# First stage of a one-layer encoder block: row scaling, transposes, the last block of w_ada and the later modulation sums

## The chip, the cores and the metric

The kernel runs on one core of a Trainium2 chip. The metric is the device time in microseconds (us). A core has TensorE (PE in the profile, with PEld for its weight loads), VectorE (DVE), ScalarE (ACT), GpSimd (POOL) and SyncE (SP). Each engine works through its own queue in order, and DMAs are issued from the queues of SP, ScalarE and GpSimd. TensorE runs at one of two levels, 1.2 or 2.4 GHz; the profile gives the granted clock as a share of the upper one.

## The reference, cut to what matters

One sequence of 1024 rows of 1024 values, all float32, one layer:

```
mod = silu(c) @ w_ada + b_ada                    # 6 pieces of 1024: shift_m, scale_m, gate_m, shift_f, scale_f, gate_f
h   = rms_norm(x, g_norm_mix) * (1 + scale_m) + shift_m
p   = h @ w_in                                   # 1024 -> 5632
z   = sigmoid(gA) * fourier(p) + sigmoid(gB) * conv(p)
x   = x + gate_m * (z @ w_o)
h2  = rms_norm(x, g_norm_moe) * (1 + scale_f) + shift_f
x   = x + gate_f * expert_choice_moe(h2)         # 16 SwiGLU experts, 128 rows each
out = rms_norm(x, g_final)
```

`rms_norm` divides each row by the root of its mean square. The change is in how `h` comes about and in the sums for the four later pieces of `mod`.

## The kernel before

The products of the block are done in parts: a float32 operand is split into two fp32r parts, the rounded value (`split`, line 94, a copy on ScalarE) and the rest (line 95, a subtraction on VectorE), and three fp32r products stand for one. A plain fp32 matmul stands in the trace as two records. The projection with `w_in` works on four quarters of `h` (two halves of the rows by two halves of the columns) and their sums.

**The ramp** (`ramp`, lines 116 to 257) makes `h`, transposed, and the first products. The rows come in eight tiles of 128 (`load_x`, line 130, into four buffers `x`), first tiles 0 to 3, later 4 to 7. For each tile `norm` squares it on ScalarE with the sum of the row as a second output (line 136), `rstd` (lines 662 to 669) takes one step on VectorE and a power on GpSimd, and VectorE makes a diagonal matrix of the 128 factors (line 139). `turn` (line 145) multiplies a 128x128 block of the tile with that diagonal on TensorE, which transposes and scales it at once; four row tiles fill one PSUM bank of two (`sm`). ScalarE takes it from there (lines 204, 221 and 241).

Beside that stands **the modulation**. `load_ada` (line 152) loads the columns of `w_ada` for shift and scale, half of them at a time, in eight blocks of 128 rows (512 KB each) through the six buffers `ld` that the blocks of `w_in` (`load_pair`, line 280) use too. `ada` multiplies each block by its column of `cact` = silu(c) and adds it to `acc` on VectorE (lines 160 and 162). `modulation` then sums `acc` over the partitions with eight fp32 products with a column of ones (line 170), and three small operations on VectorE make `shift` and `scale` (lines 173 to 175). `shape` (lines 180 to 186) applies them and splits the result, `halfprod` (line 191) runs the products. `consts` (lines 624 to 653) loads `c` and the other vectors, transposes them and computes `cact` (line 646).

The order of the program text in the ramp: `x` 0 to 3, `norm` of them, `ada(0)`, the turn of all eight column blocks, two blocks of `w_in`, `x` 4 to 7, `modulation(0)`, `shape` and products of the first quarter, `norm` of tiles 4 to 7, `ada(1)`, the turn of four column blocks and their products, two blocks of `w_in`, `modulation(1)`, and the second halves.

**The later sums.** In the gate stage `ada_rest` (lines 362 to 381) does the same for each of the other four pieces of `mod` (`q` 0 to 3): eight blocks of `w_ada` added up in `acc` on VectorE (line 372), two fp32 products of a column of ones with 512 columns of `acc` each (line 378), a copy on ScalarE (line 380) and a store to `mod_d`. Each `q` is spread over two calls of `gate`, and its products stand behind those of the second one.

What sets the order: a planner places the instructions of each engine's queue, by the program text where several are ready in its own estimate, and otherwise by readiness; a tile has to wait until a buffer of its name is free. `issue_after` pins an instruction behind another in the queue of one engine. On the chip each queue runs in the order that was planned.

Of the kernel before, what the change touches and what calls it, by code (L numbers as in the profile page):

```python
# [6 lines left out]
F32 = mybir.dt.float32  # L7
F32R = mybir.dt.float32r
# [7 lines left out]
P = 128  # L16
D = 1024
# [11 lines left out]
NSH = 0  # L29
TURN = 10  # L30
# [52 lines left out]
class Block:  # L83
# [32 lines left out]
    def ramp(self, pool, tmp):  # L116
# [11 lines left out]
        def load_x(t):  # L128
            x = tmp.tile([P, D], F32, name="x", bufs=4)
            nc.sync.dma_start(out=x, in_=io["x"][0, t * P:(t + 1) * P, :])  # L130
            return x

        def norm(x):
            sq = tmp.tile([P, D], BF16, name="sq")
            ss = pool.tile([P, 1], F32, name="ss", bufs=4)
            nc.scalar.activation(sq, x, AF.Square, accum_out=ss)
            rs = self.rstd(pool, ss, "x")
            d = pool.tile([P, P], F32, name="diag", bufs=4)
            nc.vector.tensor_scalar(d, self.ident, rs, None, op0=OP.mult)
            return x, d  # L140

        def turn(xs, k):
            ps = self.pss.tile([P, 512], F32, name="sm")
            for i, (x, d) in enumerate(xs):
                nc.tensor.matmul(ps[:, i * P:(i + 1) * P], lhsT=x[:, k * P:(k + 1) * P], rhs=d, start=True, stop=True)
# [10 lines left out]
        def ada(h):  # L156
            acc = tmp.tile([P, 2, 512], F32, name="acc", bufs=2)
            for k, w in enumerate(load_ada(h)):
                if k == 0:
                    nc.vector.tensor_scalar(acc, w, self.cact[:, 0:1], None, op0=OP.mult)  # L160
                else:
                    nc.vector.scalar_tensor_tensor(acc, in0=w, scalar=self.cact[:, k:k + 1], in1=acc,
                                                   op0=OP.mult, op1=OP.add)
            return acc

        def modulation(h, acc):
            ps = self.pss.tile([P, 512], F32, name="sm")
            for a in range(2):
                for j in range(4):
                    nc.tensor.matmul(ps[:, 4 * a + j:4 * a + j + 1], lhsT=acc[:, a, j * P:(j + 1) * P],  # L170
                                     rhs=self.ones[:, 0:1], start=True, stop=True)
            hs = slice(4 * h, 4 * h + 4)
            nc.vector.tensor_tensor(B[:, hs], ps[:, 0:4], self.bada[:, hs], op=OP.add)
            nc.vector.tensor_tensor(A[:, hs], ps[:, 4:8], self.bada[:, 8 + 4 * h:12 + 4 * h], op=OP.add)
# [187 lines left out]
    def ada_rest(self, pool, q):  # L362
# [12 lines left out]
        row = pool.tile([1, D], F32, name="acc")  # L375
        for i in range(2):
            ps = self.pss.tile([P, 512], F32, name="sm")
            nc.tensor.matmul(ps[0:1, :], lhsT=self.ones[:, 0:1], rhs=acc[:, i * 512:i * 512 + 512],
                             start=True, stop=True)
            nc.scalar.activation(row[:, i * 512:(i + 1) * 512], ps[0:1, :], AF.Copy)  # L380
# [1164 lines left out]
```

## Time and profile before

| | us |
|---|---|
| median of 3 runs | 1931.37 |
| lowest and highest of them | 1930.61, 1934.88 |
| the profiled execution | 1933.76 |
| its span in the trace | 1932.00 |
| TensorE busy in the span | 1883.5 (97%) |
| VectorE busy | 1575.3 (82%) |
| ScalarE busy | 1136.2 (59%) |
| GpSimd busy | 312.2 (16%) |

The span is the time between the first and the last instruction of the trace; 1.76 us of the profiled execution lie around it. Engines work at the same time, so the shares don't add up. A stage is bound by what ends last in it, and that is read from the chain of waits and from the busy times of the stage, not from the shares of the whole span. The ramp takes about the first 90 us, the projections go on to 490, Fourier part and mixing to about 800, the experts to the end. Matmuls are pipelined: the length of a record is longer than the distance between two of them.

### The profile page before, as it was taken

To read this page: it belongs to the slowest core of one execution; us is meant where nothing else is said; L and a number is where in the kernel's file an instruction comes from. 1 tells how busy PE (TensorE), PEld (TensorE's weight loads), DVE (VectorE), ACT (ScalarE), POOL (GpSimd) and SP (SyncE) were. 2 spreads that over 40 slices of the span, in tenths; PEclk is the share of its full clock that TensorE was granted. 3 is DMA by queue.
4 is the path that set the end of the run, shared out by engine and by line. 5 is a ranking of instruction groups with operands and counts; after the bars stand their busy time and mean duration, and the time that the engine had idled before them with its cause. 6 is when DMAs were issued, how large, how long until landed. Compare 5 with 4: busy or idle time off the path is not lost.

```text
span 1932.0 us, 24182 instructions
## 1 busy us (share of the span) xinstructions
PE 1883.5 (97%) x8777; PEld 1517.6 (79%) x8777; DVE 1575.3 (82%) x1973; ACT 1136.2 (59%) x1371; POOL 312.2 (16%) x124
## 2 busy tenths in 40 slices
PE   6999999999999999999899999999999999999996
PEld 5788888777788777877788888888888888888884
DVE  5976678676764766999898998998998998899896
ACT  5533333443510423777677776877877777777684
POOL 1000000000130110100000312321330330331231
PEclk9999999999999999999999999999999999999998
DMA  8322224466673862999899999999999999999967
GB/s 289 119 88 66 88 65 143 143 213 230 211 265 126 267 230 77 377 369 360 332 379 358 373 371 383 379 368 378 380 374 367 383 376 372 378 377 375 388 244 305
DMA packets 180236, 549.03 MB, mean 284 GB/s; under 512 B 12644, under 2 KB 51652, under 8 KB 180116
## 3 DMA queue, kind: packets, MB, share of 16 engines
q1 hardware_dynamic: 164736, 494.50, 68.3%
q0 software_dynamic: 14528, 52.75, 8.5%
q8 instruction: 69, 1.13, 0.2%
q14 instruction: 51, 0.42, 0.1%
q10 hardware_dynamic: 852, 0.24, 0.1%
HBM read 507.61 MB, written 39.86 MB: 283 GB/s over the span
## 4 chain that ended last, share of the span: by engine, by line
PE 88%; issue 4%; DVE 3%; DMA 2%; ACT 1%; POOL 1%; ACTq 0%; POOLq 0%; SPq 0%; DVEq 0%
PE a L1225 18%; PE u L1225 17%; PE y L1225 17%; PE pb L317 9%; PE pa L317 6%; PE pc L317 6%; PE mm L114 3%; PE mm L108 3%; PE mm L111 3%; PE tp L1240 1%; PE pa L191 1%; PE pb L191 1%; DMA raw<-in_w_down_e_dram 1%; DMA xg<-h_d,idx 1%; PE tp L1106 1%
## 5 line engine op out<-in xcount | busy, mean ns | idle before, releaser
L95 DVE TENSOR_TENSOR wlo<-raw,whi 128x1024 fp32r<-128x1024 f32 x759 | 883.8, 1218 | 20.3 <-ACT whi L94 18.5
L94 ACT ACTIVATE whi<-raw 128x1024 fp32r<-128x1024 f32 x759 | 777.6, 1059 | 143.5 <-PE a L1225 56.7
L1306 POOL DMA_INDIRECT x_d<-ys,idx x15 | 212.1, 14141 | 505.0 <-DVE ys L1305 479.1
L1225 PE MATMUL a<-whi,xl 128*128 128x512 f32 x512 | 162.4, 399 | 0.0
L1225 PE MATMUL a<-whi,xh 128*128 128x512 f32 x512 | 161.7, 397 | 0.2 <-ACT xh L94 0.2
L1225 PE MATMUL u<-wlo,xh 128*128 128x512 f32 x512 | 161.6, 397 | 0.0
L1225 PE MATMUL y<-whi,hth 128*128 128x512 f32 x496 | 161.4, 402 | 0.0
L1225 PE MATMUL a<-wlo,xh 128*128 128x512 f32 x512 | 161.3, 397 | 0.0
L1225 PE MATMUL u<-whi,xh 128*128 128x512 f32 x512 | 160.5, 395 | 0.0
L1225 PE MATMUL u<-whi,xl 128*128 128x512 f32 x512 | 160.3, 394 | 0.0
L1225 PE MATMUL y<-wlo,hth 128*128 128x512 f32 x496 | 157.3, 397 | 1.4 <-DVE wlo L95 1.4
L1225 PE MATMUL y<-whi,htl 128*128 128x512 f32 x496 | 157.9, 398 | 0.3 <-DVE htl L95 0.3
L94 ACT ACTIVATE wh<-s 128x512 fp32r<-128x512 f32 x80 | 50.3, 631 | 134.7 <-PE pc L317 71.4
L1225 PEld LDWEIGHTS a<-whi,xh 128*128 128x128 f32 x512 | 96.4, 189 | 22.7 <-ACT xh L94 0.5
L1225 PEld LDWEIGHTS a<-wlo,xh 128*128 128x128 f32 x512 | 96.5, 189 | 22.2
L1225 PEld LDWEIGHTS u<-whi,xl 128*128 128x128 f32 x512 | 96.4, 188 | 21.6
L1225 PEld LDWEIGHTS u<-whi,xh 128*128 128x128 f32 x512 | 96.1, 188 | 21.5
L1225 PEld LDWEIGHTS y<-wlo,hth 128*128 128x128 f32 x496 | 92.8, 188 | 25.0 <-DVE wlo L95 2.9
L1225 PEld LDWEIGHTS a<-whi,xl 128*128 128x128 f32 x512 | 95.6, 189 | 21.4 <-DVE xl L95 0.4
L1225 PEld LDWEIGHTS u<-wlo,xh 128*128 128x128 f32 x512 | 95.5, 188 | 20.8
L1225 PEld LDWEIGHTS y<-whi,htl 128*128 128x128 f32 x496 | 92.3, 188 | 21.6 <-DVE htl L95 0.7
L1225 PEld LDWEIGHTS y<-whi,hth 128*128 128x128 f32 x496 | 91.8, 188 | 20.5 <-issue 0.5
(530 smaller groups left out, 3176.1 us busy)
## 6 DMA issues: line engine op xcount, KB each, us to landing
raw<-in_w_down_e_dram SPq DMA_DIRECT2D x128, 1024.0 KB, 10.9
raw<-in_w_up_e_dram SPq DMA_DIRECT2D x126, 1024.0 KB, 7.7
raw<-in_w_gate_e_dram SPq DMA_DIRECT2D x124, 1024.0 KB, 7.0
ld<-in_w_ada_dram SPq DMA_DIRECT2D x48, 512.0 KB, 4.7
ld<-in_w_in_dram SPq DMA_DIRECT2D x44, 512.0 KB, 4.5
sg_d<-q POOLq DMA_DIRECT2D x8, 1024.0 KB, 6.0
ld<-sg_d SPq DMA_DIRECT2D x16, 512.0 KB, 4.0
x<-in_x_dram SPq DMA_DIRECT2D x8, 512.0 KB, 5.2
```

Source lines behind the costliest of these rows:

```text
L94: a = self.nc.scalar.activation(hi, src, AF.Copy).ins
L95: self.last = a, self.nc.vector.tensor_tensor(lo, src, hi, op=OP.subtract).ins
L108: nc.tensor.matmul(o, lhsT=lh, rhs=rh, start=first, stop=False)
L111: nc.tensor.matmul(o, lhsT=lh, rhs=rl, start=False, stop=False)
L114: nc.tensor.matmul(o, lhsT=ll, rhs=rh, start=False, stop=last)
L191: nc.tensor.matmul(ps, lhsT=x[:, k, :], rhs=y[:, k, :], start=first and k == 0 and i == 0, stop=not first and k == 3 and i == 2)
L317: nc.tensor.matmul(o, lhsT=x[:, k, :], rhs=y[:, k, :], start=first and k == 0 and i == 0, stop=last and k == 3 and i == 2, skip_group_chec ...
L1106: nc.tensor.transpose(pt[:, k, :], xg[:, (4 * hf + k) * P:(4 * hf + k + 1) * P], self.ident)
L1225: nc.tensor.matmul(o[:, a:b], lhsT=x, rhs=y[:, a:b], start=first and i == 0, stop=end and i == 2)
L1240: nc.tensor.transpose(pt[:, i, :], hs[q // 2][:, 512 * (q % 2) + i * P:512 * (q % 2) + (i + 1) * P], self.ident)
L1306: nc.gpsimd.indirect_dma_start(out=self.x2_d, out_offset=bass.IndirectOffsetOnAxis(ap=idx[:, 0:1], axis=0), in_=ys, in_offset=None, comput ...
```

## The change

- `consts`, `norm`: SiLU of `c` is pinned ahead of the squares on ScalarE.
- `load_x`: the buffer `x` is there seven times instead of four.
- `norm`, `turn`: instead of a diagonal on VectorE and a product with it, ScalarE scales the row tile in place, and TensorE transposes it with the identity.
- `ada`, `modulation`: VectorE adds up seven of the eight blocks of `w_ada` (`NPE` = 7). The last block goes through TensorE as it is, with its column of `cact` as the moving operand (eight fp32 products), into a PSUM tile of its own, and the products of `acc` with the column of ones into another. VectorE adds the first to `b_ada`, and the second to that.
- `ada_rest`: `acc` is split in two fp32r parts, half of the columns at a time, and each half has two fp32r products with a column of ones in fp32r instead of one in fp32.

```diff
--- before.py
+++ after.py
@@ -27,6 +27,7 @@
 NRA, NRB, NRC, NWO = 7, 4, 1, 6
 NWS, NWB = 3, 6
 NSH = 0
+NPE = 7
 TURN = 10
 NCMP = 2
 FIN = ((8, 0), (7, 2), (5, 4), (4, 6))
@@ -126,23 +127,24 @@
         B = self.cpool.tile([P, KD], F32, name="shift")
 
         def load_x(t):
-            x = tmp.tile([P, D], F32, name="x", bufs=4)
+            x = tmp.tile([P, D], F32, name="x", bufs=7)
             nc.sync.dma_start(out=x, in_=io["x"][0, t * P:(t + 1) * P, :])
             return x
 
         def norm(x):
+
             sq = tmp.tile([P, D], BF16, name="sq")
             ss = pool.tile([P, 1], F32, name="ss", bufs=4)
-            nc.scalar.activation(sq, x, AF.Square, accum_out=ss)
+            with self.tc.issue_after(self.cact_ins):
+                nc.scalar.activation(sq, x, AF.Square, accum_out=ss)
             rs = self.rstd(pool, ss, "x")
-            d = pool.tile([P, P], F32, name="diag", bufs=4)
-            nc.vector.tensor_scalar(d, self.ident, rs, None, op0=OP.mult)
-            return x, d
+            nc.scalar.activation(x, x, AF.Copy, scale=rs)
+            return x
 
         def turn(xs, k):
             ps = self.pss.tile([P, 512], F32, name="sm")
-            for i, (x, d) in enumerate(xs):
-                nc.tensor.matmul(ps[:, i * P:(i + 1) * P], lhsT=x[:, k * P:(k + 1) * P], rhs=d, start=True, stop=True)
+            for i, x in enumerate(xs):
+                nc.tensor.transpose(ps[:, i * P:(i + 1) * P], x[:, k * P:(k + 1) * P], self.ident)
             return ps
 
         def load_ada(h):
@@ -154,24 +156,31 @@
                 yield w
 
         def ada(h):
+
             acc = tmp.tile([P, 2, 512], F32, name="acc", bufs=2)
+            rest = []
             for k, w in enumerate(load_ada(h)):
                 if k == 0:
                     nc.vector.tensor_scalar(acc, w, self.cact[:, 0:1], None, op0=OP.mult)
-                else:
+                elif k < NPE:
                     nc.vector.scalar_tensor_tensor(acc, in0=w, scalar=self.cact[:, k:k + 1], in1=acc,
                                                    op0=OP.mult, op1=OP.add)
-            return acc
-
-        def modulation(h, acc):
-            ps = self.pss.tile([P, 512], F32, name="sm")
-            for a in range(2):
-                for j in range(4):
-                    nc.tensor.matmul(ps[:, 4 * a + j:4 * a + j + 1], lhsT=acc[:, a, j * P:(j + 1) * P],
-                                     rhs=self.ones[:, 0:1], start=True, stop=True)
+                else:
+                    rest.append((w, self.cact[:, k:k + 1]))
+            return rest + [(acc, self.ones[:, 0:1])]
+
+        def modulation(h, parts):
             hs = slice(4 * h, 4 * h + 4)
-            nc.vector.tensor_tensor(B[:, hs], ps[:, 0:4], self.bada[:, hs], op=OP.add)
-            nc.vector.tensor_tensor(A[:, hs], ps[:, 4:8], self.bada[:, 8 + 4 * h:12 + 4 * h], op=OP.add)
+            b = [self.bada[:, hs], self.bada[:, 8 + 4 * h:12 + 4 * h]]
+            for n, ps in enumerate((parts[:-1], parts[-1:])):
+                t = self.pss.tile([P, 512], F32, name="sm")
+                for a in range(2):
+                    for j in range(4):
+                        for i, (w, v) in enumerate(ps):
+                            nc.tensor.matmul(t[:, 4 * a + j:4 * a + j + 1], lhsT=w[:, a, j * P:(j + 1) * P], rhs=v,
+                                             start=(i == 0), stop=(i == len(ps) - 1))
+                for a, o in enumerate((B, A)):
+                    nc.vector.tensor_tensor(o[:, hs], t[:, 4 * a:4 * a + 4], o[:, hs] if n else b[a], op=OP.add)
             nc.vector.scalar_tensor_tensor(A[:, hs], in0=A[:, hs], scalar=1.0, in1=self.gmix[:, hs],
                                            op0=OP.add, op1=OP.mult)
 
@@ -373,11 +382,16 @@
             if k % 4 == 3:
                 yield
         row = pool.tile([1, D], F32, name="acc")
+        one = pool.tile([P, 1], F32R, name="one")
+        nc.vector.tensor_copy(one, self.ones[:, 0:1])
         for i in range(2):
+            cs = slice(i * 512, i * 512 + 512)
+            parts = [pool.tile([P, 512], F32R, name="acc" + x) for x in "hl"]
+            self.split(*parts, acc[:, cs])
             ps = self.pss.tile([P, 512], F32, name="sm")
-            nc.tensor.matmul(ps[0:1, :], lhsT=self.ones[:, 0:1], rhs=acc[:, i * 512:i * 512 + 512],
-                             start=True, stop=True)
-            nc.scalar.activation(row[:, i * 512:(i + 1) * 512], ps[0:1, :], AF.Copy)
+            for n, x in enumerate(parts):
+                nc.tensor.matmul(ps[0:1, :], lhsT=one, rhs=x, start=(n == 0), stop=(n == 1))
+            nc.scalar.activation(row[:, cs], ps[0:1, :], AF.Copy)
         nc.gpsimd.dma_start(out=self.mod_d[0:1, q * D:(q + 1) * D], in_=row)
 
     def conv(self, pool, n, i):
@@ -643,7 +657,7 @@
         self.col = pool.tile([P, 72], F32, name="col")
         nc.vector.tensor_copy(self.col, ps[:, 0:72])
         self.cact = pool.tile([P, 8], F32, name="cact")
-        nc.scalar.activation(self.cact, self.col[:, 0:8], AF.Silu)
+        self.cact_ins = nc.scalar.activation(self.cact, self.col[:, 0:8], AF.Silu).ins
         self.bada, self.bgate, self.wconv, self.gmix = (
             self.col[:, 8:24], self.col[:, 24:40], self.col[:, 40:64], self.col[:, 64:72])
         for n in ("ones", "neghalf", "dfte", "dfto"):
```

## Rows read from the trace of the kernel before

**Rows 1.** Busy by stage: PE, PEld, DVE, ACT, POOL us (instructions), clock, DMA share, GB/s.
```profile
370.00:430.00 60.00, 59.89 (x253) 46.81 (x252) 44.30 (x58) 24.09 (x38) 1.97 (x3) 1.00 0.60 196
...
830.00:1932.00 1102.00, 1078.41 (x4977) 868.67 (x4975) 990.85 (x1002) 817.44 (x869) 240.44 (x38) 0.99 0.96 364
```
**Rows 2.** Chain of waits from 0 to 120 us: start, length, what, instructions.
```profile
18.78 8.05 PE sm L145 x48
26.82 1.75 PE sm L170 x16
...
28.86 0.17 DVE scale L175
...
54.68 1.69 PE sm L170 x16
...
60.82 2.54 PE pa L191 x6
```
**Rows 3.** Busy time by stretches of the ramp, columns as in rows 1.
```profile
9.00:22.00 13.00, 8.11 (x31) 6.93 (x32) 8.09 (x14) 7.32 (x13) 3.13 (x4) 1.00 1.05 382
...
24.00:27.00 3.00, 3.00 (x29) 3.00 (x28) 1.03 (x1) 1.93 (x4) 0.00 (x0) 1.00 0.02 6
...
18.80:23.60 4.80, 4.80 (x22) 4.80 (x23) 4.69 (x4) 1.61 (x3) 0.00 (x0) 1.00 1.05 357
...
31.30:37.40 6.10, 6.10 (x14) 4.59 (x15) 4.37 (x10) 6.04 (x12) 1.10 (x2) 0.50 1.01 377
...
58.20:60.80 2.60, 0.97 (x4) 0.48 (x3) 2.60 (x6) 2.60 (x5) 0.00 (x0) 1.00 0.66 196
60.80:64.70 3.90, 3.88 (x10) 3.05 (x11) 3.90 (x7) 3.26 (x6) 0.00 (x0) 0.57 0.02 8
...
86.10:91.60 5.50, 5.50 (x25) 4.43 (x25) 5.47 (x13) 3.13 (x5) 0.00 (x0) 1.00 0.60 194
```
**Rows 4.** SP's queue in order of time: start, from first to last issue, what, issues.
```profile
18.46 1.69 SPq L280 DMA_DIRECT2D ld<-in_w_in_dram  x2
26.18 1.77 SPq L130 DMA_DIRECT2D x<-in_x_dram  x4
28.05 15.34 SPq L152 DMA_DIRECT2D ld<-in_w_ada_dram  x8
...
97.91 0.30 SPq L368 DMA_DIRECT2D acc<-in_b_ada_dram  x1
```
**Rows 5.** ScalarE's groups, 0 to 60 us: operation, count | busy us, mean ns | idle before.
```profile
L136 ACT ACTIVATE sq<-x 128x1024 bf16<-128x1024 f32 x8 | 8.4, 1052 | 0.2
...
L94 ACT ACTIVATE wh<-ld 128x512 fp32r<-128x512 f32 x7 | 4.0, 616 | 0.0
...
L136 ACT ACTIVATION_READ_ACCUMULATOR sq<-x 128x1 f32 x8 | 1.5, 187 | 0.0
L136 ACT ACT_TABLE_LOAD x1 | 1.3, 1283 | 7.4 <-DMA vrow<-in_b_gate_dram 7.4
```
**Rows 6.** VectorE's groups, 0 to 60 us, columns as in rows 5.
```profile
L162 DVE SCALAR_TENSOR_TENSOR acc<-ld,cact,acc 128x1024 f32<-128x1024 f32 x14 | 17.9, 1280 | 0.2
L95 DVE TENSOR_TENSOR wl<-ld,wh 128x512 fp32r<-128x512 f32 x6 | 4.0, 687 | 0.0
```
**Rows 7.** Chain of waits around the first later sum, 355 to 372 us.
```profile
362.36 2.78 PE pb L317 x12
365.14 1.81 PE sm L378 x4
366.95 2.98 PE pa L317 x12
```
**Rows 8.** Chain of waits ahead of the second later sum, 395 to 410 us.
```profile
403.50 3.05 PE pb L317 x12
```
**Rows 9.** TensorE in order of time near 657 us.
```profile
657.59 0.60 PE L746 MATMUL mm<-ident,ld 128*128 128x128 f32 x4
```
**Rows 10.** Line 746, transposes of 128x128: length of a record in ns, min/median/max.
```profile
L746 PE MATMUL mm<-ident,ld x64: 270/272/329, 657.6 to 763.0; 128*128 128x128 f32 x64
```

## The prediction

> **What bounds the kernel now.** I read four views, in this order. The busy table by stage comes first [rows 1]: TensorE is busy 59.89 of 60 us in a stretch of the gate stage and 98% of the time in the experts, while DMA carries 196 GB/s in the first and 364 GB/s in the second. So behind the ramp a microsecond of TensorE work is a microsecond of span, and a microsecond that the ramp gives back is carried to the end, because the weight stream of the experts starts later or sooner together with the rest. Only the ramp (the first 60 us) has stretches that wait. The chain of waits shows which [rows 2]: the turning of the rows (L145, over at 26.8), the column sums of the modulation (L170), then VectorE's `scale` at 28.86, and only then products. The same pattern comes a second time: L170 at 54.68, then products from 60.82. The reader is to see in it that the products of each half hang on a modulation, and the modulation on eight blocks of `w_ada`. Third, the stretches of the ramp [rows 3]: from 9 to 22 us DMA runs at 382 GB/s with a busy share of 1.05, so a block of 512 KB takes 0.524 MB / 382 = 1.37 us, and the blocks come one behind the other until the queue is dry (6 GB/s from 24 to 27; I set the landing of its last block at 24.6). Fourth, the issue order on SP [rows 4].
>
> The same stretches tell the clock. One record of an fp32 matmul took 4.80/22 = 0.218 us between 18.8 and 23.6 (1.2 GHz by its pace), against 1.75/16 = 0.109 in L170 at 26.82 (2.4 GHz). After the pause around 29 us the granted clock was 0.50 from 31.3 to 37.4, though TensorE was busy for all 6.10 us of it; half of that, 3.05 us, is lost. After the second pause (58.2 to 60.8, busy 0.97 of 2.60) it was 0.57 over 3.90 us, a loss of 1.7 us.
>
> **SiLU first, rows scaled on ScalarE.** One of the two table loads goes (1.28 us, [rows 5]), and `cact` is ready at 7.4 + 1.28 + 0.2 = 8.9 us. The diagonal products leave VectorE; that is worth nothing by itself. ScalarE gets a scaling of 128x1024 for each row tile. No such operation is in the trace; the square of the same size is, at 1.05 us, and I take that for it. Four squares with their reads (1.05 + 0.19) and four scalings make 9.2 us, so the last tile is scaled at about 18.1 us. The old turn of the first column blocks was done by 18.78; what this comes later is hidden, since the turn isn't what ends last, as the next two parts show.
>
> **Transposes.** A 128x128 fp32 product is two records, a transpose one. At the high clock four of those in L746 lie 0.11 us apart ((0.60 - 0.27)/3, the 0.27 being one record's length, [rows 9, 10]). At the low clock none of this size is shown; bounds are 0.11 and 0.22, and I take 0.22, as every record near it doubled. In the first half 8 x 4 transposes then need about 0.9 us a column block, with ScalarE's shorter evacuation beside it, and end near 24 us instead of 26.8. The second half is on TensorE's path: 32 products of two records (64 x 0.109 = 7.0 us) become 32 x 0.11, **-3.5 us**.
>
> **The first modulation.** SP's order decides here. `x` gets seven buffers, so the loads of row tiles 4, 5 and 6 wait for no buffer any more, while blocks 6 and 7 of `w_ada` wait for one of six `ld` buffers, which block 0's sum gives back. The order within a queue is not that of the program text: the load of `b_ada` for a sum of the gate stage stands at 97.91 on SP, among the weight loads of the second pair, because it waits for nothing [rows 4]. So I expect the three `x` loads in front of blocks 6 and 7. In the old run two blocks of `w_in` stood behind block 7 [rows 4], so that one landed at 24.6 - 2 x 1.37 = 21.9; it would now land 3 x 1.37 = 4.1 us later, at 26.0. VectorE's sum over seven blocks then ends one block and one sum behind, 24.6 + 1.28 = 25.9 [rows 6]. Behind that TensorE has 16 records for block 7 and 16 for `acc`, where 16 were before.
>
> At which clock? Between 18 and 24 us transposes half as long as the old products leave the array idle in half of the time, and from 24 to 26 nothing runs. In the rows the clock rose only after 4.80 us of unbroken fp32 products, and it stayed down from 31.3 on for several microseconds with TensorE fully busy [rows 3]. I take the low clock: 32 x 0.215 = 6.9 us, `scale` at 26.0 + 6.9 + 0.4 = 33.3 instead of 29.0: **+4.3 us**. The bounds are -2.3 (no load passes, high clock: turn over at 22.8, 32 x 0.109 = 3.5, plus 0.4) and +9 (below, the slower rival).
>
> The Trainium skill bears on this, TensorE: Matmul & The Clock Gate, Part 4: PE-mode transpose: it says that transposes don't count as activity for the clock as matmuls do. No run here shows it, since the transposes of the trace stand in fours between dense products. By that rule the sum stays as it is; were they to count like the old products, the first modulation would cost 3.4 us less and the time would be 1923.0.
>
> **The second half.** The products start 4.3 us later with the same low clock at their head (0, with 1.7 us either way, as the rise can come earlier or later within them). But the blocks of `w_ada` for the second half no longer start at 28.05, behind four `x` loads that waited for the end of the turn [rows 4]; three of the four are gone from there, and DMA needn't run dry. Behind the 14 blocks that the old run had by 24.6 stand 12 more, which end at 24.6 + 12 x 1.37 = 41.0; the old last issue was at 28.05 + 15.34 = 43.4. VectorE has one block less (1.28) and four diagonals less, so I expect the second `acc` some 6 us sooner than the old one, whose sums began at 54.68, and the second `scale` before 55, ahead of the end of the products in front of it (36 + 36 products at 0.232 [rows 7], 16 transposes, the low clock: about 57 us). The second modulation has 16 records more on TensorE's path, **+1.75 us**. Then the pause goes with its clock: **-2.6 - 1.7 = -4.3 us**. What is late next is TensorE itself; VectorE, busy 5.47 of 5.50 us from 86.1 on [rows 3], comes next, about as much sooner as `scale` is.
>
> **Later sums.** Four times two fp32 products of 128x512 take 1.81 us, and in three cases the product behind takes 2.98 instead of 2.78 [rows 7]: 4 x 1.81 + 3 x 0.20 = 7.8 us. Sixteen fp32r products at 2.78/12 = 0.232 take 3.7: -4.1. The splits (0.62 on ScalarE, 0.69 on VectorE for each half, [rows 5, 6]) lie beside products: VectorE is busy 74% there [rows 1]. The part buffers are single, so the second split waits for the first products; on TensorE the next gate's products stand behind these and can fill the time if the planner puts some of them between, on VectorE its weight splits stand behind the part's subtraction. VectorE is not free in every place, though: at 403.50 twelve products took 3.05, because a weight split was late [rows 8]. I count 0.2 us a sum for that, and take **-3.3 us** (bounds -4.1, and +1.5 if each sum waits a whole second split, 1.4 us).
>
> **Sum:** +4.3 - 3.5 + 1.75 - 4.3 - 3.3 = -5.0 us (rounded). The profiled execution took 1933.76 (span 1932.00), and would take 1928.8. It lies 2.4 above the median; from the median, 1931.37, the forecast is **1926.4 us**.
>
> **Rivals.**
> 1. The first modulation is not late. For it: SP's planned order can't be seen in the trace, and the clock of transposes can't either. Against it: [rows 4] with `b_ada`. Clock up: -3.4, 1923.0; loads in place, low clock (turn over at 24, `scale` at 31.3): -2.1, about 1924.3; both: 1919.8.
> 2. The second pause stays, since the last `x` tile still waits for the end of the turn and stands ahead of the `w_ada` blocks on SP, or VectorE takes the sums between its splits as slowly as before. Then the 4.3 us are not won: 1930.7.
> 3. Slower: the second half's rows get in front of the first half's on ScalarE too. Three tiles at 1.05 + 0.19 + 1.05 = 2.3 us are 6.9 us in front of the evacuations of the turn, which then ends near 31; 6.9 us of modulation behind it make `scale` late by 9 us (another +4.9), the last `x` load and the blocks behind it go out late, and the second pause stays (+4.3): -5.0 + 9.2 = +4.2, 1935.6. It decides once the first `scale` is later than about 37. Against it: evacuations come earlier in the program.
> 4. The change doesn't do what it says in the later sums: the parts wait for their splits as long as they save. -5.0 + 3.3: 1929.7.
>
> **Chances.** Forecast 0.38, rivals 0.28, 0.18, 0.09, 0.07. The forecast's own range is 1923.5 to 1930. The range of 8 in 10 reaches from the better cases of rival 1 to a little above rival 2: 1918.5 to 1932. A measurement of this kernel can tell about 0.2%, 3.9 us: faster than 1927.5 are two thirds of the forecast's case, and nearly all of rival 1, 0.55; slower than 1935.2 is rival 3, 0.09; the rest, 0.36.
>
> **What would show it.** Right: three `x` loads on SP before the seventh `w_ada` block; the 32 records of the first modulation starting near 26 and 0.21 us apart; the first `scale` at 33 and the second before 55; no pause of TensorE near 58 and no low clock behind it; 0.93 us for each later sum. Wrong: blocks 6 and 7 issued right behind block 5, a first `scale` before 30, a pause that stays, TensorE waiting for the parts of a sum.

## The result, and the profile after

| | before | after |
|---|---|---|
| median, first comparison (4 runs each) | 1933.12 | 1946.47 |
| ratio, with its 95% interval | | 1.0060, 1.0043 to 1.0076 |
| median, second comparison (33 and 10 runs) | 1936.05 | 1946.35 |
| ratio, with its 95% interval | | 1.0052, 1.0035 to 1.0068 |
| the profiled execution, its span | 1933.76, 1932.00 | 1945.12, 1943.3 |

The changed kernel is slower by 0.5 to 0.6%, 10 to 13 us; the forecast was 5 us faster. Line numbers of after are larger: the scaling is L141, the transposes L147, the one-column products L180, `scale` L184, the products of the ramp L200, the later sums L393, the splits L95 and L96.

The chain of waits of after, 15 to 75 us (start, length, what, instructions), answers to [rows 2]:

```profile
17.48 1.55 POOL xrs L682
19.05 1.16 ACT x L141
...
21.41 5.40 PE sm L147 x24
26.82 4.20 PE sm L180 x32
31.31 0.17 DVE scale L184
...
45.04 1.55 POOL xrs L682
46.62 1.16 ACT x L141
...
51.54 0.97 PE pa L200 x3
...
59.48 3.48 PE sm L180 x32
...
63.81 0.07 DVE scale L184
...
67.41 2.93 PE pa L200 x6
```

The turn still ends at 26.8; it begins later, because the last row tile is scaled only at 20.2, and that waited for GpSimd. `scale` is 2.45 us late. Before the second turn the same chain (GpSimd, ScalarE) stands in front of TensorE, and the products behind the second modulation begin at 67.41 instead of 60.82. Stretches of after (columns as in rows 1) answer to [rows 1, 3]:

```profile
31.30:35.60 4.30, 0.01 (x1) 0.02 (x1) 3.18 (x7) 4.03 (x7) 0.00 (x0) 0.50 0.87 322
35.60:41.70 6.10, 6.10 (x17) 4.80 (x18) 3.44 (x8) 5.75 (x9) 1.54 (x2) 0.63 0.36 97
...
64.00:70.90 6.90, 5.14 (x11) 3.64 (x12) 6.87 (x13) 5.52 (x9) 0.00 (x0) 0.51 0.51 156
...
480.00:560.00 80.00, 76.54 (x368) 61.42 (x367) 53.36 (x92) 33.64 (x52) 9.49 (x11) 0.96 0.66 217
```

TensorE stands still for all 4.3 us of the first stretch, the second pause and its low clock are still there, and a new stretch has idle time and a low clock: the Fourier part from 480 on. The first product in TensorE's order of time (start, length, line, operation, count, idle time before it and what ended it), and ScalarE's order around it:

```profile
26.82 1.95 PE L180 MATMUL sm<-cact,ld 128*128 128x1 f32 x16
28.62 2.38 PE L180 MATMUL sm<-ones,acc 128*128 128x1 f32 x16
35.59 0.80 PE L200 MATMUL pa<-11h,wh 128*128 128x512 f32 x1 [4.58 <-ACT wh L95]
```

```profile
31.57 0.81 ACT L193 ACTIVATE 11h<-hf,shift,scale 128x512 fp32r<-128x512 f32 x1 [4.12 <-DVE scale L184]
...
34.92 0.61 ACT L95 ACTIVATE wh<-ld 128x512 fp32r<-128x512 f32 x1
```

The product waits for the split of `w_in`, which the planner put behind five operations of `shape`; ScalarE had been idle for 4.12 us in front of them. In the kernel before, the split stood ahead of `shape`, and the first product came at 29.98, with no wait for it. ScalarE's and TensorE's order of time there:

```profile
27.35 0.62 ACT L94 ACTIVATE wh<-ld 128x512 fp32r<-128x512 f32 x1
```

```profile
29.98 0.49 PE L191 MATMUL pa<-11h,wh 128*128 128x512 f32 x1 [1.42 <-ACT 11h L184]
```

SP's queue of after (start, from first to last issue, what, issues) answers to [rows 4], and ScalarE's groups, 0 to 70 us, to [rows 5]:

```profile
6.54 9.31 SPq L154 DMA_DIRECT2D ld<-in_w_ada_dram  x8
16.83 2.17 SPq L289 DMA_DIRECT2D ld<-in_w_in_dram  x2
19.05 7.65 SPq L131 DMA_DIRECT2D x<-in_x_dram  x4
26.80 19.77 SPq L154 DMA_DIRECT2D ld<-in_w_ada_dram  x8
```

```profile
L141 ACT ACTIVATE x<-x,xrs 128x1024 f32<-128x1024 f32 x8 | 9.1, 1144 | 4.6 <-POOL xrs L682 4.6
```

No `x` load passed a `w_ada` block. The first three `x` loads are issued from 19.05 on, but the fourth goes out only at the end of the turn (the four issues end at 26.70), and the second half's blocks stand behind it: they start at 26.80 instead of 28.05 and are issued over 19.77 us instead of 15.34. A scaling takes 1.14 us (taken: 1.05), and ScalarE waited 4.6 us for GpSimd in front of the eight. The later sums, in the chain around 371 and 410 us, answer to [rows 7, 8]:

```profile
371.55 0.47 PE sm L393 x2
372.02 0.70 PE pa L326 x3
372.72 0.29 PE sm L393
373.01 0.93 PE pa L326 x4
373.94 0.23 PE sm L393
```

```profile
409.46 3.06 PE pb L326 x12
```

A sum takes 0.47 + 0.29 + 0.23 = 0.99 us of TensorE instead of 1.81, with products between; the late weight split of [rows 8] (3.05) is still there, at 3.06. Behind the gates, the chain of after around 504 us, and ScalarE's order of time in the kernel before:

```profile
503.88 0.28 ACT rlh L95
504.17 0.95 ACT coshi L95
...
505.17 0.80 PE mm L109
```

```profile
487.80 1.04 ACT L94 ACTIVATE coshi<-ld 128x1024 fp32r<-128x1024 f32 x1
...
493.32 1.05 ACT L94 ACTIVATE coshi<-ld 128x1024 fp32r<-128x1024 f32 x1
```

`coshi` is the rounded part of the cosine table. It is split in two halves. Before, the first half ran between operations of the last gate and the second between the channel splits, with the first product that needs it at 497.02. After, both stand behind the channel splits, and TensorE waits for it until 505.17.

So the delay of the same product, after minus before, is +5.6 us at the first product, +5.8 at the first product behind the ramp (91.5 in the kernel before), +5.1 at the last gate product, +3.7 at the first channel product, +8.1 at the first cosine product, +10.6 at 539, and +11.3 in the span.

**How far two traces can be compared.** The granted clock falls in the two pauses of the ramp, in the Fourier part, in some traces further on (near 640 to 670), and early in the experts (near 920), and not in the same way in each execution. Busy time times one minus the granted clock, summed over slices of 1 us, is the time lost to it:

| lost to the clock, us | 50 to 95 | 480 to 540 |
|---|---|---|
| before | 1.70 | 0.00 |
| after, two executions | 2.55, 2.94 | 3.02, 5.64 |
| one kernel of the experiments (e14, e17), two executions | 0.00, 1.67 | 3.42, 1.71 |
| scaled rows alone; SiLU alone | 3.93; 1.71 | 5.11; 3.41 |

The trace of before is one that lost nothing in the Fourier part; it is the only one of the 19 traces that lost nothing from 480 to 830, the others lost 1.6 to 7.2 us there. Some 3 us of a difference between two traces can be this alone. The ramp differs as well: three kernels of the experiments leave the ramp as it was (e1, e5, e10), and their traces reach the product of 91.5 3.5, 0.3 and 2.9 us sooner than the trace of before. So the verdicts below go by the medians, and the traces are used for places and waits.

### The profile page after: what moved, and what is told of

It reads as the page before. It is cut to its first block, busy times and chain, and to the rows that moved or that the text cites. A ratio compares the mean times of both kernels' runs of the same rounds, so it can differ in the third digit from the quotient of the medians.

```text
span 1943.3 us, 24128 instructions
## 1 busy us (share of the span) xinstructions
PE 1879.3 (97%) x8745; PEld 1514.3 (78%) x8745; DVE 1577.1 (81%) x1979; ACT 1147.5 (59%) x1386; POOL 315.6 (16%) x124
## 4 chain that ended last, share of the span: by engine, by line
PE 84%; DVE 5%; issue 5%; DMA 4%; ACT 2%; POOL 1%; ACTq 0%; POOLq 0%; SPq 0%; DVEq 0%
PE a L1239 17%; PE y L1239 17%; PE u L1239 17%; PE pb L326 7%; PE pa L326 5%; PE pc L326 5%; PE mm L115 3%; PE mm L109 3%; PE mm L112 3%; DMA ld<-in_w_ada_dram 2%; PE tp L1254 1%; DMA xg<-h_d,idx 1%; DMA raw<-in_w_down_e_dram 1%; PE pa L200 1%; PE tp L1120 1%
## 5 line engine op out<-in xcount | busy, mean ns | idle before, releaser
L96 DVE TENSOR_TENSOR wlo<-raw,whi 128x1024 fp32r<-128x1024 f32 x759 | 883.7, 1217 | 20.9 <-ACT whi L95 18.5
L95 ACT ACTIVATE whi<-raw 128x1024 fp32r<-128x1024 f32 x759 | 777.6, 1059 | 144.2 <-PE a L1239 56.8
L95 ACT ACTIVATE wh<-s 128x512 fp32r<-128x512 f32 x80 | 50.2, 631 | 128.1 <-PE pc L326 69.5
```

The source lines that it names most:

```text
L95: a = self.nc.scalar.activation(hi, src, AF.Copy).ins
L96: self.last = a, self.nc.vector.tensor_tensor(lo, src, hi, op=OP.subtract).ins
```

## The experiments

Ratios are to the kernel before on the same chip, with the 95% interval; 0.1% is 1.9 us.

**The parts alone.** Each run is the kernel before with one part of the diff shown above. The later sums:

```diff
+            self.split(*parts, acc[:, cs])
...
+                nc.tensor.matmul(ps[0:1, :], lhsT=one, rhs=x, start=(n == 0), stop=(n == 1))
```

> The kernel before with the later sums in two fp32r parts, nothing else of the change. In the changed kernel the gate stage gained only 0.6 us, and the Fourier stage behind it lost 7 to 8.6 us: its cos products waited 2.88 us for ScalarE's split of the cos table (line 94), which had stood between the gate operations at 487.8 and 493.3 before, and now came behind the channel splits. Theory A, the new sums move that split in the planned order: the whole loss in the Fourier stage is there in this kernel too, cos products 7 to 9 us later than before while the gates end at the same time or 0.6 us sooner; span +6 to +8 us. Rival B, the Fourier loss comes from the ramp's delay (the table lands or is split at another time against the gates): no loss here, -0.6 to -3.3 us.

Measured: 1.0011 (1.0001 to 1.0022). In its trace the first cosine product waits 2.88 us for `coshi`, and its delay against before rises by 4.4 us between the first channel product and the first cosine product. Theory A for the place and the wait. Its size was too high: the 2 us that the sums themselves gain stand against it, and the expectation took the Fourier part of the changed kernel, with its low clock, for the price of the place. The clock fell inside the wait here too (at 495.4).

The scaled rows and transposes:

```diff
+            nc.scalar.activation(x, x, AF.Copy, scale=rs)
...
+                nc.tensor.transpose(ps[:, i * P:(i + 1) * P], x[:, k * P:(k + 1) * P], self.ident)
```

> The kernel before with rows scaled on ScalarE and transposed as they are, nothing else. Theory A, two causes of the ramp's +5.8 us of the changed kernel: the scaling puts a chain ScalarE, VectorE, GpSimd, ScalarE in front of each transposed row tile, which is hidden in the first half and delays the second half's products (starved from 46.2 to 51.5 in the changed kernel). Here the first scale then stands at 28.5 to 30, the first product at 30 to 31, and the second half's products start 0 to 6 us later than before; the span is between 0 and +3 us. Rival B, the row part is the saving it was forecast to be (-3.5 us in the second half): -2 to -4 us. Rival C, the row part makes the whole ramp loss: +5 to +6.

Measured: 1.0013 (1.0002 to 1.0023), first product at 30.63. Theory A. TensorE's order of time in it before the products of the second half:

```profile
43.70 0.44 PE L145 MATMUL sm<-ident,x 128*128 128x128 f32 x2 [1.49 <-ACT x L139]
45.51 0.69 PE L145 MATMUL sm<-ident,x 128*128 128x128 f32 x2 [1.37 <-ACT x L139]
46.85 1.97 PE L145 MATMUL sm<-ident,x 128*128 128x128 f32 x8 [0.65 <-ACT hg L221]
```

The last block of `w_ada` through TensorE:

```diff
+                elif k < NPE:
...
+                    rest.append((w, self.cact[:, k:k + 1]))
```

> The kernel before with the last block of w_ada through TensorE in the modulation, nothing else. Theory A: 16 more records in front of scale (1.75 us), less one sum of VectorE (1.28) if that ended last, and the first product waits for the split of w_in on ScalarE, which now stands behind the operations of shape (first product 4.6 us behind the second modulation in the changed kernel, 1.1 us before): first scale at 28.9 to 30.7, first product 2 to 4 us later than before, span +2 to +4. Rival B, the split's place costs nothing by itself and the ramp's loss comes from the rows: first product within 1 us of before, span within 1 us.

Measured: 1.0023 (1.0011 to 1.0035), `scale` at 30.30, first product at 34.57, idle 4.58 for the split. Theory A, and the dearest part by its ratio, though the intervals of the three overlap.

SiLU first, and the seven buffers:

```diff
+            with self.tc.issue_after(self.cact_ins):
```

> The kernel before with SiLU of c pinned ahead of the squares, nothing else. Theory A: one table load (1.28 us) less on ScalarE, sums of VectorE may begin sooner, but the first modulation hangs on the last block's landing: span within 0.5 us of before. Rival B, the pin holds the squares back until c has landed and so delays the turn of the rows: first scale 1 to 2 us later, span +1 to +2.

```diff
+            x = tmp.tile([P, D], F32, name="x", bufs=7)
```

> The kernel before with seven buffers x instead of four and nothing else. The loads of row tiles 4 to 6 then start some 7 us sooner, behind the w_in blocks on SP, and DMA doesn't run dry. Theory A, nothing waits for them there: 0.9985 to 1.0005. Rival B, they take DMA time from the w_in blocks or hold the w_ada blocks of the second half back: over 1.001. Rival C, the w_ada blocks of the second half land sooner and the second modulation comes 2 us or more sooner: 0.998 or less.

Measured: 0.9998 (0.9981 to 1.0014) and 0.9993 (0.9976 to 1.0010). Neither moves the time. The whole again:

> The changed kernel again, timed in more rounds beside the kernel before. The four parts alone cost +2.1 (sums), +2.5 (rows), +4.5 (block through TensorE) and 0 us (SiLU) by their ratios, 9 us in sum. Theory A, the parts add up: ratio 1.004 to 1.006. Rival B, they share their losses (the ramp's delay of the rows and that of the modulation lie one beside the other): 1.002 to 1.004; or, C, they hinder each other: over 1.006.

Measured: 1.0052. Theory A by the medians: the five parts sum to 1.0038, which lies in the interval of the whole (1.0035 to 1.0068). The intervals are too wide to tell whether the rows and the block share a part of their loss: at the product of 91.5 their traces are 3.6 and 4.7 us late, and the two traces of the whole 5.8 and 6.3.

**The cosine table.** Two idle tiles in the gates' pool, and nothing of the change:

```diff
+        for x in "hl":
+            nc.vector.memset(pool.tile([P, 512], F32, name="acc" + x)[0:1, 0:1], 0.0)
```

> The kernel before, with two tiles of 128x512 more in the pool of the gate stage, of which one value is set to zero on VectorE; nothing of the change. Theory A, in the later sums alone the split of the cos table came late because the part tiles take space that the table's tile got while the gates still ran: here too that split stands behind the channel splits, the cos products come 4 to 6 us late against the gates' end, and the span is 3 to 5 us longer than that of the kernel before. Rival B, the late split comes from the work of the sums on ScalarE: with two idle tiles nothing moves, span within 1 us.

Measured: 1.0033 (1.0018 to 1.0047), medians 1943.29 and 1936.05. Its TensorE and ScalarE in order of time:

```profile
498.90 0.80 PE L108 MATMUL mm<-coshi,veh 128*128 128x512 f32 x1 [3.61 <-ACT coshi L94]
```

```profile
497.62 0.28 ACT L94 ACTIVATE rlh<-rl 1x96 fp32r<-1x96 f32 x1 [1.36 <-DVE rl L495]
497.81 1.99 ACT L94 ACTIVATE coshi<-ld 128x1024 fp32r<-128x1024 f32 x2
```

Theory A: 4 KB per partition of tiles that nothing uses cost 6 to 7 us (3.5 to 9.1 by the interval), more than the 3 to 5 that were expected. From the first channel product to the first cosine product this trace loses 4.1 us; the clock fell at 496.5, inside the wait. How much of the low clock behind it the wait brought isn't shown, since kernels without the wait lose clock in the Fourier part too. The other way round, the sums with their parts in buffers that are there anyway:

```diff
-            parts = [pool.tile([P, 512], F32R, name="acc" + x) for x in "hl"]
+            parts = [self.wsp.tile([P, 512], F32R, name="w" + x) for x in "hl"]
```

> As the run with the later sums alone, but their parts stand in the buffers of the weight parts (wh, wl, six of each) instead of two new tiles in the pool of the gate stage. In the run before this one the cos products came 4.4 us late against the end of the gates (shift -5.65 at the first channel product, -1.21 at the first cos product), because the split of the cos table stood on ScalarE behind all channel splits. Theory A, the new tiles cause that (they take space or time that the table's split had): with them gone, the split of the cos table stands before the last gate operation again (within 1 us of the gates' end) and the cos products keep the lead of the gates; span 3 to 5 us shorter than that of the sums alone, 1 to 3 us under the kernel before. Rival B, the sums move the table's split by what they put on ScalarE, wherever the parts stand: the cos products still wait some 4 us for it, span as with the sums alone (+2).

Measured: 0.9970 (0.9954 to 0.9986). ScalarE's order of time:

```profile
485.45 1.04 ACT L94 ACTIVATE coshi<-ld 128x1024 fp32r<-128x1024 f32 x1
...
492.46 1.04 ACT L94 ACTIVATE coshi<-ld 128x1024 fp32r<-128x1024 f32 x1
```

The two halves stand where they stood before, the first between the gate's operations, the second between the channel splits. Theory A for the place; the gain on the sums with tiles of their own (1.0011), 0.41% or 8 us, is larger than the 3 to 5 us expected. In this trace the gates gain 2.1 us by the last product and 3.1 by the first channel product.

**The split of `w_in`.**

```diff
+        first = self.last[0]
         for k in range(4):
-            shape(hf[:, k, :], k, b["11"])
+            with self.tc.issue_after(first):
+                shape(hf[:, k, :], k, b["11"])
```

> As the run with the last block of w_ada through TensorE alone, but the first split of w_in on ScalarE is pinned ahead of the operations of shape, as it stood in the kernel before. There the first product came at 34.57, 4.27 us behind scale (30.30), against 1.12 us in the kernel before. Theory A, this split's place is most of the part's loss: the first product comes 1.1 to 1.7 us behind scale, at about 31.5, and the ramp's delay falls from 4.7 to 1.5 to 2 us, which is what the 16 more records take; span 2 to 4 us shorter than without the pin. Rival B, VectorE's or ScalarE's operations of shape are what ends last, and the split was only the last in a row that is late anyway: the first product stays 3 us or more behind scale, and the span stays.

Measured: 1.0004 (0.9987 to 1.0021). TensorE in order of time:

```profile
26.04 1.87 PE L179 MATMUL sm<-cact,ld 128*128 128x1 f32 x16
27.77 2.20 PE L179 MATMUL sm<-ones,acc 128*128 128x1 f32 x16
31.40 0.80 PE L199 MATMUL pa<-11h,wh 128*128 128x512 f32 x1 [1.43 <-ACT 11h L192]
```

Theory A: the first product is 1.1 us behind `scale` (30.27), 3.2 us sooner than without the pin. By the ratios most of the part's loss is gone, though the two intervals overlap.

**The chain of the rows.** First attempt, the squares of tiles 4 to 6 ahead of `shape`:

```diff
+        xs[:3] = [square(x) for x in xs[:3]]
...
+            with self.tc.issue_after(xs[2][2]):
+                shape(hf[:, k, :], k, b["11"])
```

> As the run with the scaled rows alone, with seven buffers x, and with the squares of row tiles 4 to 6 pinned on ScalarE ahead of the first operation of shape, where ScalarE waits for scale. Theory A, the second half starts late because its chain of square, mean, power and scaling stands behind shape on ScalarE (last scaling at 44.3, starved from 42 to 46 there): the last scaling comes at 40 or before, TensorE isn't starved between the two halves, the products of the second half begin 4 to 6 us sooner than without the pin, and the ramp is 0 to 3 us faster than in the kernel before instead of 3.6 slower. Rival B, the last row tile, whose load waits for the end of the turn, sets the start of the second half whatever stands on ScalarE: no more than 1 us sooner. Rival C, the squares in front of shape delay the first product as much as they bring the second half forward: first product 2 us or more later, end of the ramp as before.

Measured: 1.0006 (0.9991 to 1.0022), first product at 36.30. Inconclusive: the planner put a scaling between the squares, which waited for GpSimd, and `shape` stood behind it. The changed kernel with all three mends, this order of the rows among them:

> The changed kernel with all three: the first split of w_in pinned ahead of shape, the squares of tiles 4 to 6 pinned ahead of shape, the parts of the later sums in the buffers of the weight parts. Theory A, the three places account for most of the loss of 11.3 us: -3 (first product), -3 to -5 (second half), -4 (cos table), so the span is 1932 to 1935, within 0.2% of the kernel before. Rival B, the places are symptoms and the changed kernel's ramp is bound by the longer modulation and the chain of the rows in any order: span 1938 or more.

Measured: 1.0001 (0.9987 to 1.0014), span 1937.2. Between the two theories; nearly all the loss is gone, but not in all three places. The ramp is no better: the same scaling stands between the squares and waits 4.71 us for GpSimd, the first product comes at 38.96 (35.59 in the changed kernel), and the product of 91.5 is 5.6 us late (5.8 in the changed kernel). What was won lies behind the ramp, where the buffers of the parts alone are worth 0.41%. This run doesn't show that the ramp's two mends work together; the later run of the whole change in the second order (e16) has that product 2.2 us late. The turn with products by the identity instead of transposes:

```diff
-                nc.tensor.transpose(ps[:, i * P:(i + 1) * P], x[:, k * P:(k + 1) * P], self.ident)
+                nc.tensor.matmul(ps[:, i * P:(i + 1) * P], lhsT=x[:, k * P:(k + 1) * P], rhs=self.ident, start=True, stop=True)
```

> The kernel before with the rows scaled on ScalarE, but turned by fp32 products with the identity instead of transposes: two records for one. The prediction gave the transposes 3.5 us of the second half. Theory A, the second half of that kernel waits for scaled rows, not for the turn, so that most of what the transposes are shorter by is lost in waiting: 0 to 1.5 us slower than the scaled rows with transposes. Rival B, the transposes do bring their 3.5 us, and the chain of the scaling costs that and more: 3 to 4 us slower than with transposes, first modulation 1 to 2 us later as well.

Measured: 1.0025 (1.0010 to 1.0039), 2.3 us over the scaled rows with transposes, between the two theories, and the intervals overlap. The place is clear: the turn ends at 30.0 instead of 26.8, and the first product comes at 33.35 instead of 30.63. So the transposes bring the first product 2.7 us forward, where they make good the late scaling; what of that lasts to the end isn't shown. Second attempt at the order:

```diff
+        xs[:2] = [square(x) for x in xs[:2]]
...
+        with self.tc.issue_after(xs[1][2]):
+            w[0, 0] = split_w(0, 0, 0)
...
+        with self.tc.issue_after(shaped):
+            xs[2:] = [square(x) for x in xs[2:]]
+            xs = [norm(*x) for x in xs]
```

> As the scaled rows alone, with seven buffers x, but only the squares of row tiles 4 and 5 ahead of shape on ScalarE (and ahead of the first split of w_in), and all four scalings pinned behind shape. Theory A, the rows lose by where their chain stands and not by its length: first product 0.5 to 1.5 us later than in the kernel before, the last scaling by 42 (44.3 to 45.5 before), TensorE not starved between the halves, the products of the second half 1 to 3 us sooner than in the kernel before: ratio 0.998 to 0.9995, where the scaled rows alone had 1.0013. Rival B, VectorE's sums and GpSimd's powers behind them set the start of the second half whatever the order on ScalarE: last scaling at 44 or later, ratio 1.0005 to 1.0015.

Measured: 0.9987 (0.9975 to 0.9999). Theory A; the first product comes at 30.93, the last scaling ends at 42.1, and TensorE goes from the first half into the turn without a wait:

```profile
43.29 0.39 PE L192 MATMUL pc<-11h,wl 128*128 128x512 f32 x1
43.52 1.03 PE L146 MATMUL sm<-ident,x 128*128 128x128 f32 x8
```

**Put together.** The sums in the other buffers with SiLU first, and with the second order of the rows on top (timed twice):

> The kernel before with the later sums in two parts that stand in the buffers of the weight parts, and SiLU pinned first. The first alone had a ratio of 0.997. Theory A, SiLU first brings the first modulation 0.7 to 0.9 us forward, as with SiLU alone: 0.9965. Rival B, it brings nothing that lasts, as its own ratio (0.9998) says: 0.997.

> The same order of the rows, with the later sums in the buffers of the weight parts and SiLU first (these two alone had 0.9971). Theory A, the gains add up: 0.995 to 0.9966. Rival B, the rows bring nothing in any order: 0.997 to 0.998.

> The same without the block on TensorE, timed again beside it: 0.994 to 0.9965, as before.

Measured: 0.9971 (0.9956 to 0.9986); then 0.9948 (0.9930 to 0.9966) and 0.9942 (0.9921 to 0.9963). Rival B of the first: SiLU first brings nothing that lasts. Theory A of the second: the gains add up (0.9971 and 0.9987 make 0.9958), and a little more. This version beats both kernels, medians 1929.04 and 1928.69 against 1937.29 and 1939.22. With the block of `w_ada` on TensorE as well:

> The whole change, with the order mended in three places: squares of tiles 4 and 5 and the first split of w_in ahead of shape and the scalings behind it, and the parts of the later sums in the buffers of the weight parts. Without the block of w_ada on TensorE this order had a ratio of 0.9948. Theory A, the 16 records more in each modulation (1.75 us at the high clock, 3.4 at the low one) lie on TensorE's path, and VectorE's block less brings nothing: 0.9958 to 0.9975. Rival B, the block less on VectorE pays for the records: 0.9940 to 0.9955.

Measured: 0.9971 (0.9958 to 0.9984). Theory A: the whole change in a good order is 5.7 us faster than before by the medians of its comparison, and without that block 10.5. In this trace the 32 records take 5.4 us (16 in 2.06, 16 in 3.55), `scale` stands at 32.7 instead of 29.2 without the block, and the 16 records more of the second modulation take 1.95. With the pin alone the block had cost 0.8 us (-2.5 to 4.1), here it costs 4.9, so its price in a good order is not settled; no order shown makes it a gain.

## Why the prediction was wrong

By place in the two profiled traces: the ramp, forecast at 4.3 - 3.5 + 1.75 - 4.3 = -1.75 us, came out at +5.8. The later sums, forecast at -3.3, won 2.1 by the first channel product (+5.8 to +3.7). Behind them the forecast had nothing, and 7.6 were lost (+3.7 to +11.3), 4.4 of them up to the first cosine product. The steps that failed, term by term:

- **The first modulation, +4.3.** The step that failed first: "I expect the three `x` loads in front of blocks 6 and 7". SP kept the order of the text; `b_ada` [rows 4] was no model for it. What the forecast had right, a start of the 32 records near 26, was luck: they began at 26.82, behind the end of the turn and not behind a late block. The turn didn't end near 24, since the forecast counted the scaling of the rows by ScalarE's own time (18.1) and not by its chain: two of four powers took 1.6 us instead of 0.55, and the last scaling ended at 20.2. The clock was high when the 32 records began and fell under them, 4.20 us where 6.9 were taken. So `scale` stood at 31.3, 2.0 sooner than forecast. What ended last then was the split of `w_in` on ScalarE, 3.2 us more, which the working didn't look for: ScalarE's order around the edit was not followed, only its times.
- **The transposes, -3.5.** Right as a time of TensorE (eight in 1.03 us at the high clock, 0.11 apart); but TensorE didn't end last there. The squares and scalings of tiles 4 to 7, which the working had on ScalarE only, became the path of the second half (idle for `x` in the scaled rows alone). In the second order the rows bring 2.5 us (0.9987, 0.2 to 4.8 us by the interval).
- **The 16 records, +1.75.** Right for the second modulation: 3.48 against 1.69.
- **The second pause, -4.3.** Rival 2 came true, by its first reason: the fourth `x` load waited for the end of the turn, and the blocks behind it started only 1.25 us sooner (26.80). The pause stayed, since the second `scale` didn't come before 55 but at 63.8, and the low clock behind it stayed too (64.0 to 70.9 at 0.51).
- **The later sums, -3.3.** Right as a time of TensorE, 0.99 us a sum against 0.93 forecast; of the term the changed kernel's gates won 0.6 us by their last product and 2.1 by the first channel product, and with the parts elsewhere 2.1 and 3.1 (0.9970 in the whole, 2.7 to 8.9 us). The failed step is what the split was said to cost: only its engines and its own single buffers were weighed, not the space of the two new tiles. These two tiles are what moved the split of the cosine table, 6 us by the padded kernel. That the table's tile gets space which a gate tile still holds is the likely way; no run shows addresses.
- **Rival 3** named ScalarE, crowded by the second half's rows, but at the first `scale`; it is the start of the second half that they delay. None of the rivals had the Fourier part.
- **The range** took its bounds from the ramp and the sums, and had nothing for a changed order in stages that the diff doesn't touch.

The rule that was weighed, the Trainium skill, TensorE: Matmul & The Clock Gate, Part 4: PE-mode transpose, that transposes don't count for the clock, did not hold here: TensorE ran only transposes from 11.85 to 26.8, and the records behind them went 0.11 us apart at once. The 3.4 us that this was to give were partly had (4.20 in place of 6.9) and then lost behind the split. The prediction read the low clock of 18.8 to 23.6 by its pace, while the row gives 1.00 there: the clock record of a trace begins with its first rise (at 23.77 before, at 26.51 after), and the rows give 1.00 for all time ahead of that.

## What to carry to other kernels

With a planner that places each queue, an edit is priced by the order that it makes, not only by its instructions: look at what stands in front of the next product on every engine before and after, in the stages behind the edit as well. A new tile is not free, even one that nothing uses: here two of them moved a split in the next stage. Put short-lived parts into buffers that are there. When a large change loses, time its parts alone and then mend the order of each: here the same work was 0.5% slower in one order, and 0.3% faster in another order with the parts in other buffers.

## What the runs showed of the hardware

**GpSimd waits for VectorE.** The powers of after on GpSimd and VectorE's sums beside them, both in order of time:

```profile
15.60 1.62 POOL L682 TENSOR_TENSOR xrs<-xms,neghalf 128x1 f32<-128x1 f32 x1 [3.94 <-DVE xms L680]
17.48 1.54 POOL L682 TENSOR_TENSOR xrs<-xms,neghalf 128x1 f32<-128x1 f32 x1 [0.27 <-DVE xms L680]
38.47 0.55 POOL L682 TENSOR_TENSOR xrs<-xms,neghalf 128x1 f32<-128x1 f32 x1 [19.46 <-DVE xms L680]
```

```profile
15.52 1.28 DVE L166 SCALAR_TENSOR_TENSOR acc<-ld,cact,acc 128x1024 f32<-128x1024 f32 x1
```

A power of one column takes 0.55 us alone. One that starts behind the start of a sum ends 0.42 us after the sum's end (15.52 + 1.28 = 16.80, 15.60 + 1.62 = 17.22); so does the next, beside the sum that starts at 17.32 (18.60 and 19.02). The Trainium skill, SBUF — State Buffer, section "SBUF: two separate sides", says that the two engines share a pair of ports that one of them holds for a whole instruction; the trace agrees.

**The clock rose behind transposes and fell under one-column products.** Stretches of after (columns as in rows 1):

```profile
29.00:30.00 1.00, 1.00 (x10) 1.00 (x11) 0.03 (x1) 0.00 (x0) 0.00 (x0) 0.96 1.02 340
30.00:31.00 1.00, 1.00 (x5) 0.92 (x5) 0.00 (x0) 0.00 (x0) 0.00 (x0) 0.50 1.04 342
```

The transposes ahead of 26.8 lie 0.21 us apart. Behind them the 16 records at 26.82 took 1.95 us (0.11 apart, 2.4 GHz by their pace); the next 16, without a gap between them, took 2.38, as the clock fell at 29.9 under them, to 0.50. In another kernel (e14) the transposes themselves go from 0.21 to 0.11 us apart, at 25.8, with only transposes on TensorE from 12 on. In the whole change in the better order the second 16 took 3.55, all at the low clock.

**A busy TensorE can lose its clock.** In the scaled rows alone (e2), Fourier part (columns as in rows 1):

```profile
504.00:508.00 4.00, 4.00 (x25) 3.61 (x24) 2.31 (x8) 3.33 (x5) 0.00 (x0) 0.75 0.70 264
508.00:512.00 4.00, 4.00 (x13) 3.09 (x14) 3.88 (x13) 2.45 (x7) 0.00 (x0) 0.50 0.78 252
```

It is busy in every microsecond, and at the lower level (1.2 GHz) from 506.0 to 512.8. Directly ahead of the fall ran products with two columns (L685, 504.4 to 505.7) and the first channel products of a group (L481, 66 columns). The trace of before, with the same products at 501.1 to 503.5, has 1.00 there.
